# Feed-forward of a hybrid decoder layer: sum rows on another queue, scaling in place, other PSUM banks at the start of the second pair

## The chip, the core and the metric

The kernel runs on one core of one Trainium2 chip. The core has five engines that run their own instruction streams and meet through semaphores: TensorE (PE, matmuls), VectorE (DVE), ScalarE (ACT), GpSimd (POOL) and SyncE (SP). Each engine works in the order of its own program. SP and POOL here mostly issue transfers (DMAs). The metric is device time in microseconds, from the executions' own clock; lower is better. All values are float32.

## The reference, cut to what matters

One decoder layer works on a prompt of 2048 tokens and on 8 x 4 sample tokens. Two parallel branches (a gated linear recurrence and sliding-window attention) are merged by gates and multiplied by `w_o`; then comes the feed-forward, which is where the change lies, and a last norm:

```python
x = x + m @ w_o
h2 = _rmsnorm(x, n2)
x = x + jnp.square(jax.nn.relu(h2 @ w_ff1)) @ w_ff2
...
y_prompt = _rmsnorm(xp, normf_w)
y_sample = _rmsnorm(xs, normf_w)
```

Here x is tokens x 1024, `w_ff1` is 1024 x 4096 and `w_ff2` 4096 x 1024; `_rmsnorm` divides each token's row by the root of its mean square and multiplies by a weight.

## The kernel before

**Blocks and pairs.** The tokens stand in four blocks, features on the 128 partitions, tokens along the row. Two neighbouring blocks make a pair, and the feed-forward works on pairs: pair 0 with 512 columns per block (one chunk), pair 1 with 528 (two chunks of 264). The stages run one after another: projections and both branches of all blocks, `w_o` (tile `wob`), then for pair 0 the first feed-forward product (f1) and the second (f2), then f1 and f2 of pair 1.

**Seven products.** Both feed-forward matrices are multiplied by Strassen's scheme: the two blocks of a pair are the rows and the two halves of the features the columns of a 2 x 2 matrix. It needs the input halves A11, A12, A22 and four sums of them, S1 to S4. The function `ff_sums` makes the sums: for each of four row groups k it loads the pieces a11, a21, a12, a22 (from the DRAM buffers h2d, already normed, and x1d, not yet scaled) into one tile `xo`, scales what came from x1d (L598), writes one of the scaled pieces back to h2d (L600), forms s1, s2, s3, s4 with four DVE operations (L605 to L608) and stores them to the DRAM buffers dS (L610). The next k uses the same `xo`. For pair 1 this is done inside f2 of pair 0, in its second step. Its loads are L594 (from h2d) and L596 (from x1d); where a piece lies in both buffers there are two loads.

**Split numbers.** Every operand is split into a high and a low part, an ACT cast (L151, L257) and a DVE subtraction (L152, L258), and each product is three matmuls: high by high, high by low, low by high (L264 to L266 in f1, L1580 to L1582 in f2). So a weight tile such as `lw2T` goes DMA, ACT cast to `hw2T`, DVE subtraction in place, PE.

**f1.** `strassen_T` runs over 16 pairs of weight columns; each with each chunk is a `Unit`. Six units (pair 0) or ten (pair 1) begin ahead with two products (`a`: tiles fB, fC), and after each a list of `hooks` adds other work. Then every unit takes its remaining products (`b`, `c`), which use weights w1T and the sums. A unit's PSUM banks come from one of two rings of two banks, mm or tp; units 0 and 1 take mm, 2 and 3 tp, and so on. In pair 0 the norm of the last block (`Norm.stat`, tile `n_fb`: eight PE transposes of a sum of squares, a DVE reduction, a POOL power; then `spread`) is among the work that lies beside the first units. In pair 1 the hooks finish the output of pair 0's second block: squares, the statistic (`n_y`, PSUM ring hg), `spread`, and `Fin.out`, which scales eight rows of y by the norm (L1441) and writes them out (L1442, POOL's queue). There `f1.o` gives the scaled rows two buffers of their own, `fx_o`. The last of these hooks also loads S4, into the operand slot in which y stands, and `mid` splits it after unit 0's `b`.

**f2.** The second product has seven steps of four groups g; a group takes two weight tiles (`rw2B` or `lw2T`, L1558, SP's queue), one stored activation (`f2A` or `f2S`, L1574, SP's queue), and, in pair 0, 48 matmuls. After each step DVE adds the PSUM banks to y (L1587). For pair 0 the last step uses the hg and mm rings.

**What sets the order.** A scheduler in the kernel's framework takes instructions by priority and data dependences, within each engine; `pin` keeps an instruction in the order in which the program states it. The order on an engine is then fixed, and an instruction whose semaphore is not there holds up all behind it on that engine. This holds for transfers too: SP's queue carries weights, activations and the loads of `ff_sums` in one order; POOL's queue carries the stores and the loads of S1 to S4 (L615).

Of the kernel before, what the change touches and what calls it, by code (L numbers as in the profile page):

```python
# [16 lines left out]
P = 128  # L17
# [26 lines left out]
def tile_hybrid_step(  # L44
# [163 lines left out]

    def stat(rs, sq, n, name, ring=tp_ps):

        w = WT[n]
        nt = n // w
        for t0, ln in chunks_of(n):
            ps = ring(f"n_{name}_{t0}")[0:w].rearrange("p (c e) -> p c e", e=P)[:, 0:ln // w]
            for i in range(ln // w):
                nc.tensor.transpose(ps[:, i], sq[:, t0 + i * w:t0 + (i + 1) * w], ident)
            nc.vector.tensor_reduce(rs[:, t0 // w:(t0 + ln) // w], ps, AX.X, ALU.add)
        nc.vector.tensor_scalar(rs, rs, 1.0 / D, EPS, ALU.mult, ALU.add)
        nc.gpsimd.tensor_tensor(rs, rs, negh[0:w].broadcast_to([w, nt]), ALU.pow)
# [11 lines left out]
    class Norm:  # L231


        def __init__(u, tmp, n, w, name):
            u.tmp, u.n, u.w, u.N, u.acc = tmp, n, w, name, None
            u.rs, u.ring = carry_rs[0:WT[n], 0:n // WT[n]], tp_ps

# [9 lines left out]
        def stat(u):  # L247
            stat(u.rs, u.acc, u.n, u.N, u.ring)

# [60 lines left out]
    class Unit:  # L310


        def __init__(u, idx, w, t0, ln, A, st, fin):
            u.n, u.w, u.t0, u.ln, u.N = w.n, w.ops, t0, ln, f"{w.N}_{t0}"
            u.free = False
            u.ring, u.pair, u.A, u.st_, u.fin = (mm_ps, tp_ps)[idx // 2 % 2], w, A, st, fin

# [56 lines left out]

    def strassen_T(N, npairs, src, chunks, A, st, fin, ahead, early, mid, free, wt):
        ws = [Wpair(N, n, src, wt) for n in range(npairs)]
        nch = len(chunks)
        units = [Unit(i, ws[i // nch], *chunks[i % nch], A, st, fin) for i in range(npairs * nch)]
        if free:
# [205 lines left out]
    def ff_sums(b, v, r, k, loaded=False, q=nc.gpsimd):  # L585
# [4 lines left out]
        for x, (r0, c0) in zip(r, () if loaded else ((0, 0), (4, 0), (0, Th), (4, Th))):  # L590
            rows = slice((r0 + k) * P, (r0 + k + 1) * P)
            cut = min(max(raw0 - c0, 0), Th) if b == nsb - 1 else Th
            if cut:
                nc.sync.dma_start(x[:, 0:cut], h2d[b][rows, c0:c0 + cut])  # L594
            if cut < Th:
                nc.sync.dma_start(x[:, cut:Th], x1d[b][rows, c0 + cut:c0 + Th])  # L596
                i = c0 + cut - raw0
                nc.vector.scalar_tensor_tensor(x[:, cut:Th], x[:, cut:Th], n2c[:, r0 + k:r0 + k + 1], carry[:, i:i + Th - cut], ALU.mult, ALU.mult)  # L598
            if b == nsb - 1 and r0 and c0:
                nc.gpsimd.dma_start(h2d[b][rows, c0:c0 + Th], x)  # L600
# [31 lines left out]
    for bi in range(nblk):  # L632
# [774 lines left out]
        if last_b:  # L1407
            n2.ring = sw_ps
        late += [n2.stat, n2.spread] + ([] if last_b else [h2_out])
# [35 lines left out]
    for sb in range(nsb):  # L1445
# [13 lines left out]
        with tc.tile_pool(name=f"f1_{sb}", bufs=1, reuse_waits="tile") as fp:  # L1459
# [13 lines left out]
            else:  # L1473
                f1.x = lambda r: carry[:, 0:f1.ln] if r in ("acc", "rb") else fp.tile([P, f1.ln], F32, tag="fs", bufs=2, name=f"fx_{r}")
                f1.ns = lambda name: carry_rs
                f1.o = lambda: f1.x("o")
                hooks = [[lambda: f1.sq(0, 1, 2, 3)], [lambda: f1.sq(4, 5, 6, 7)], late_ops[0:2] + [f1.stat], late_ops[2:4], [f1.spread], [lambda: f1.out(0, 1, 2, 3)],
# [8 lines left out]
            def mid(u):  # L1486
                for f in s4_load:
                    f(u.c12)

# [3 lines left out]
            def f1_fin(u, blk, x, ps=None):  # L1493
# [12 lines left out]
                for o, y_ in (("A11", u.c11), ("A12", u.c12), ("A22", u.c22), ("S1", s1), ("S2", s2), ("S3", s3), ("S4", s4)):  # L1506
# [4 lines left out]
                       lambda ln, name: fp.tile([P, ln], F32, tag="st", bufs=12 * len(chunks), name=name),  # L1511
                       f1_fin, 6 if len(chunks) == 1 else 10, early, mid, True, lambda dt, name: fp.tile([P, 1024], dt, tag="we", bufs=2, name=name))

# [236 lines left out]
```

## Time and profile before

| | |
|---|---|
| median of three runs | 2822.58 us (2820.04 to 2824.71) |
| profiled execution, first to last instruction | 2810.0 us |
| TensorE clock granted, mean | 0.993 |
| transfers | 487.60 MB, mean 174 GB/s |
| f1 of pair 0 | from about 1499 us |
| f2 of pair 0 | about 1810 to 2122 us |
| f1 of pair 1 | from 2124 us |

The profile is of one execution; for its time the page gives only the span from the first to the last instruction, and the runs' times include what lies before and after it. The views used are: the busy time of each engine; the chain of waits that ended last; the timeline (start, length, engine, line, operation, and in brackets the idle time before it and what ended it); the waits, summed by line and by what was waited for; and windows, which give each engine's busy time in a stretch. In a name such as `lw2T_021` the digits are pair, group and half. Tiles lose these digits in the trace's views.

### The profile page before, as it was taken

The page shows a single profiled execution, that of the slowest core. Times are in us where ns is not written, and L with a number is a line of the kernel's source. Part 1 is how long each engine was busy: PE and PEld are TensorE (multiplying, and loading weights), DVE is VectorE, ACT ScalarE, POOL GpSimd, SP SyncE. Part 2 cuts the span into 40 slices and gives each one's busy share as a digit, 9 for nine tenths or more (in the row PEclk, how much of TensorE's full clock was granted, in tenths as well). Part 3 has the DMA queues.
Part 4 walks back from the last instruction along what each step waited for, and adds up shares of the span by engine and source line. Part 5 has one row for each costly group of instructions (what it writes and reads, how often), then busy time and mean ns, then how long its engine had stood idle before and what let it go on. Part 6 is the DMA issues. An engine that isn't in the chain of part 4 may idle for free.

```text
span 2810.0 us, 50089 instructions
## 1 busy us (share of the span) xinstructions
PE 2730.1 (97%) x20053; PEld 2403.9 (86%) x20053; DVE 1791.2 (64%) x2905; ACT 1110.0 (40%) x2070; POOL 490.9 (17%) x782
## 2 busy tenths in 40 slices
PE   8999999999999999899999999999999999999998
PEld 7778888788899977677898888878888999999998
DVE  5675746746774385637667777765567777654556
ACT  4542445423344353335334333434344233343332
POOL 1100211002300102320231221220012343320001
PEclk9999999999999999999999999999999999999999
DMA  5237662377743424652365544796566444485553
GB/s 190 75 103 237 208 198 76 97 242 256 251 126 115 144 76 149 219 160 67 105 210 184 181 145 150 265 317 222 190 200 215 147 161 135 155 291 184 189 187 119
DMA packets 344481, 487.60 MB, mean 174 GB/s; under 512 B 23432, under 2 KB 220824, under 8 KB 344248
## 3 DMA queue, kind: packets, MB, share of 16 engines
q1 hardware_dynamic: 289112, 329.10, 37.5%
q0 software_dynamic: 42880, 140.22, 13.8%
q10 hardware_dynamic: 12256, 15.08, 1.5%
q8 instruction: 157, 2.57, 0.4%
q14 instruction: 76, 0.62, 0.1%
HBM read 353.64 MB, written 130.68 MB: 172 GB/s over the span
## 4 chain that ended last, share of the span: by engine, by line
PE 78%; DMA 6%; DVE 6%; issue 5%; ACT 2%; POOL 2%; SPq 0%; POOLq 0%; DVEq 0%; ACTq 0%
PE f L1581 6%; PE f L1582 6%; PE f L1580 6%; PE fB_f L264 4%; PE fB_f L266 3%; PE fB_f L265 3%; PE fD_f L264 2%; PE fD_f L266 2%; PE fD_f L265 2%; PE ps_hfb L684 2%; PE fB_z L264 1%; PE fB_z L266 1%; PE fB_z L265 1%; PE wob L1390 1%; PE gab L166 1%
## 5 line engine op out<-in xcount | busy, mean ns | idle before, releaser
L1582 PE MATMUL f<-f2S,lw2T 128*128 128x264 f32 (+1 forms) x576 | 184.4, 320 | 2.0 <-DVE lw2T L152 2.0
L1580 PE MATMUL f<-f2S,hw2T 128*128 128x264 f32 (+1 forms) x576 | 184.5, 320 | 1.6 <-ACT hw2T L151 1.6
L1581 PE MATMUL f<-f2S,hw2T 128*128 128x264 f32 (+1 forms) x576 | 184.0, 319 | 0.0
L264 PE MATMUL fB_f<-S,w1T_f 128*128 128x264 f32 (+1 forms) x384 | 123.2, 322 | 3.1 <-ACT c_f L327 2.2
L152 DVE TENSOR_TENSOR lw2T<-lw2T,hw2T 128x1024 fp32r<-128x1024 f32 x64 | 78.2, 1224 | 69.7 <-ACT hw2T L151 68.8
L265 PE MATMUL fB_f<-S,w1T_f 128*128 128x264 f32 (+1 forms) x384 | 122.5, 319 | 0.0
L1580 PE MATMUL f<-f2A,h_w2B 128*128 128x264 f32 (+1 forms) x384 | 122.4, 319 | 0.0
L1581 PE MATMUL f<-f2A,h_w2B 128*128 128x264 f32 (+1 forms) x384 | 122.3, 319 | 0.0
L1582 PE MATMUL f<-f2A,l_w2B 128*128 128x264 f32 (+1 forms) x384 | 122.3, 318 | 0.0
L266 PE MATMUL fB_f<-S,w1T_f 128*128 128x264 f32 (+1 forms) x384 | 122.0, 320 | 0.0
L151 ACT CAST hw2T<-lw2T 128x1024 fp32r<-128x1024 f32 x64 | 67.2, 1051 | 137.2 <-DMA lw2T<-w_T 137.2
L1582 PEld LDWEIGHTS f<-f2S,lw2T 128*128 128x128 f32 x576 | 108.4, 188 | 10.4 <-DVE lw2T L152 2.9
L1580 PEld LDWEIGHTS f<-f2S,hw2T 128*128 128x128 f32 x576 | 108.8, 189 | 9.9 <-ACT hw2T L151 2.4
L1388 PE MATMUL wob<-m_b,h_wob 128*128 128x512 f32 (+2 forms) x320 | 113.1, 353 | 3.2 <-ACT h_wob L257 3.2
L1390 PE MATMUL wob<-m_b,l_wob 128*128 128x512 f32 (+2 forms) x320 | 112.4, 353 | 3.0 <-DVE l_wob L258 2.8
L1581 PEld LDWEIGHTS f<-f2S,hw2T 128*128 128x128 f32 x576 | 108.8, 189 | 7.6
L1389 PE MATMUL wob<-m_b,h_wob 128*128 128x512 f32 (+2 forms) x320 | 112.5, 352 | 0.0
L152 DVE TENSOR_TENSOR f2S<-f2S 128x1024 fp32r<-128x1024 f32 (+1 forms) x64 | 78.9, 1240 | 41.3 <-ACT f2S L151 40.9
L257 ACT CAST w1T_f<-w1r_f 128x512 fp32r<-128x512 f32 x128 | 77.1, 619 | 69.7 <-DVE w1r_f L300 29.7
L258 DVE TENSOR_TENSOR w1T_f<-w1r_f,w1T_f 128x512 fp32r<-128x512 f32 x128 | 87.4, 688 | 26.0 <-ACT w1T_f L257 25.7
L1507 POOL DMA_DIRECT2D u_A<-c_f x106 | 57.4, 541 | 236.1 <-DVE c_f L1491 225.1
L1507 POOL DMA_DIRECT2D u_S<-s_f x144 | 77.7, 541 | 109.0 <-DVE s_f L1502 92.4
(845 smaller groups left out, 9256.8 us busy)
## 6 DMA issues: line engine op xcount, KB each, us to landing
w1r_f<-w_ff SPq DMA_DIRECT2D x64, 512.0 KB
lw2T<-w_T SPq DMA_DIRECT2D x64, 512.0 KB
rw2B<-w_ff SPq DMA_DIRECT2D x48, 512.0 KB
f2S<-u_S SPq DMA_DIRECT2D x32, 528.0 KB
ws<-w_ff SPq DMA_DIRECT2D x32, 512.0 KB
r_wob<-w_o SPq DMA_DIRECT2D x32, 512.0 KB
f2S<-u_S SPq DMA_DIRECT2D x32, 512.0 KB
u_S<-s_f POOLq DMA_DIRECT2D x96, 132.0 KB, 2.3
```

The costliest lines, as they stand in the source:

```text
L152: pin(nc.vector.tensor_tensor(lo, F(lo), F(hi), ALU.subtract), on)
L258: pin(nc.vector.tensor_tensor(dl, src, F(dh), ALU.subtract), on)
L264: nc.tensor.matmul(ps, wh, ah, start=(first and k == 0), stop=False, skip_group_check=not first)
L265: nc.tensor.matmul(ps, wh, al, start=False, stop=False, skip_group_check=not first)
L266: nc.tensor.matmul(ps, wl, ah, start=False, stop=(last and k == 3), skip_group_check=not first)
L1388: nc.tensor.matmul(p, wh, ah, start=(k == 0), stop=False)
L1389: nc.tensor.matmul(p, wh, al, start=False, stop=False)
L1390: nc.tensor.matmul(p, wl, ah, start=False, stop=(k == KD - 1))
L1507: nc.gpsimd.dma_start(us[o][u.n // 4][u.n % 4 * P:(u.n % 4 + 1) * P, u.t0:u.t0 + u.ln], y_)
L1580: nc.tensor.matmul(ps, wh, ah, start=first, stop=False, skip_group_check=cont)
L1581: nc.tensor.matmul(ps, wh, al, start=False, stop=False, skip_group_check=cont)
L1582: nc.tensor.matmul(ps, wl, ah, start=False, stop=lastk, skip_group_check=cont)
```

## The change

Five edits, of which two go together.

- The loads of `ff_sums` are issued on POOL's queue, not SP's.
- The transposes of the last block's statistic in pair 0 are pinned (`n2.on`).
- `f1.o` goes: `Fin.out` scales pair 0's second block in place, in y, and writes y out.
- In pair 1 the units take the two PSUM rings the other way round (`flip`): units 0 and 1 take tp, 2 and 3 mm.
- The splits of S4 in pair 1 are pinned (`on=True`).

```diff
-    def stat(rs, sq, n, name, ring=tp_ps):
+    def stat(rs, sq, n, name, ring=tp_ps, on=False):
...
-                nc.tensor.transpose(ps[:, i], sq[:, t0 + i * w:t0 + (i + 1) * w], ident)
+                pin(nc.tensor.transpose(ps[:, i], sq[:, t0 + i * w:t0 + (i + 1) * w], ident), on)
...
-            u.rs, u.ring = carry_rs[0:WT[n], 0:n // WT[n]], tp_ps
+            u.rs, u.ring, u.on = carry_rs[0:WT[n], 0:n // WT[n]], tp_ps, False
...
-            stat(u.rs, u.acc, u.n, u.N, u.ring)
+            stat(u.rs, u.acc, u.n, u.N, u.ring, u.on)
...
-            u.ring, u.pair, u.A, u.st_, u.fin = (mm_ps, tp_ps)[idx // 2 % 2], w, A, st, fin
+            u.ring, u.pair, u.A, u.st_, u.fin = (mm_ps, tp_ps)[(idx // 2 + flip) % 2], w, A, st, fin
...
             if cut:
-                nc.sync.dma_start(x[:, 0:cut], h2d[b][rows, c0:c0 + cut])
+                nc.gpsimd.dma_start(x[:, 0:cut], h2d[b][rows, c0:c0 + cut])
             if cut < Th:
-                nc.sync.dma_start(x[:, cut:Th], x1d[b][rows, c0 + cut:c0 + Th])
+                nc.gpsimd.dma_start(x[:, cut:Th], x1d[b][rows, c0 + cut:c0 + Th])
...
         if last_b:
-            n2.ring = sw_ps
+            n2.ring, n2.on = sw_ps, True
...
-                f1.o = lambda: f1.x("o")
...
             def mid(u):
                 for f in s4_load:
-                    f(u.c12)
+                    f(u.c12, on=True)
...
-                       f1_fin, 6 if len(chunks) == 1 else 10, early, mid, True, lambda dt, name: fp.tile([P, 1024], dt, tag="we", bufs=2, name=name))
+                       f1_fin, 6 if len(chunks) == 1 else 10, early, mid, True, lambda dt, name: fp.tile([P, 1024], dt, tag="we", bufs=2, name=name), sb)
```

The line that goes makes every line number behind it one lower in the changed kernel (L1506 there is L1507 before).

**The start of f1 of pair 0.** PE, from the last matmuls of `w_o` (`wob`) to unit 0 (`fB_f_0`, `fC_f_0`); `n_fb` is the statistic, - is before:

```order
 L1389 MATMUL wob_288_14941<-m_b_14230,h_wob_14934 128x256
 L1390 MATMUL wob_288_14941<-m_b_14230,l_wob_14935 128x256
-L216 MATMUL n_fb_0_15178<-ident,carry 68x128 x4
-L216 MATMUL n_fb_272_15184<-ident,carry 68x128 x4
 L264 MATMUL fB_f_0_0_15100<-A_0_14652,w1B_f_0_15093 128x512
 L265 MATMUL fB_f_0_0_15100<-A_0_14652,w1B_f_0_15093 128x512
 L264 MATMUL fC_f_0_0_15115<-A_0_14661,w1B_f_0_15097 128x512
```

The eight transposes leave this place. PE further on, between the end of unit 1's and the start of unit 2's products:

```order
 L265 MATMUL fC_f_1_0_15163<-A_0_14661,w1B_f_1_15145 128x512
 L266 MATMUL fC_f_1_0_15163<-A_0_14661,w1B_f_1_15145 128x512
+L216 MATMUL n_fb_0_15178<-ident,carry 68x128 x4
+L216 MATMUL n_fb_272_15184<-ident,carry 68x128 x4
 L264 MATMUL fB_f_2_0_15201<-A_0_14652,w1B_f_2_15194 128x512
 L265 MATMUL fB_f_2_0_15201<-A_0_14652,w1B_f_2_15194 128x512
```

They now stand two units later. The reductions on DVE and the power on POOL follow them.

**The second step of f2 of pair 0.** SP before, in the third and fourth group of the step (`lw2T_02`, `lw2T_03`: weights; `f2S`: activations; `xo`: the sum rows of k=2 and k=3):

```order
L1558 DMA lw2T_020_17953<-w_T_139 128x2x512
L1574 DMA f2S_0_18033<-u_S_3_0_15075 128x2x512 x2
L1558 DMA lw2T_021_17958<-w_T_139 128x2x512
L596 DMA xo_17493<-x1d_101 128x528
L594 DMA xo_17493<-h2d_103 128x512
L596 DMA xo_17493<-x1d_101 128x16
L596 DMA xo_17493<-x1d_101 128x528
L1558 DMA lw2T_030_18041<-w_T_139 128x2x512
L1574 DMA f2S_0_18102<-u_S_0_0_15084 128x2x512 x2
L1558 DMA lw2T_031_18046<-w_T_139 128x2x512
L594 DMA xo_17493<-h2d_103 128x512
L596 DMA xo_17493<-x1d_101 128x16
```

All L594 and L596 rows leave SP's queue (24 transfers), so weights follow activations there without a break. POOL now, at the change from k=1 to k=2 (`dS_1_108` to `111`: the stores of S1 to S4):

```order
L610 DMA dS_1_109<-xo_17493 128x528
L610 DMA dS_1_110<-xo_17493 128x528
L594 DMA xo_17493<-h2d_103 128x512
L596 DMA xo_17493<-x1d_101 128x16
L596 DMA xo_17493<-x1d_101 128x528 x2
L610 DMA dS_1_111<-xo_17493 128x528
L600 DMA h2d_103<-xo_17493 128x528
L594 DMA xo_17493<-h2d_103 128x512
L596 DMA xo_17493<-x1d_101 128x16
L610 DMA dS_1_108<-xo_17493 128x528
```

Before, POOL had only the L610 and L600 rows here. Now each load stands behind stores of the k before, and the last store of k=1 (`dS_1_111`) stands behind three loads of k=2. DVE before, around the low part of `lw2T_021`:

```order
L152 TENSOR_TENSOR lw2T_020_17953<-lw2T_020_17953,hw2T_020_17952 128x1024
L606 TENSOR_TENSOR xo_17493<-xo_17493 128x528
L152 TENSOR_TENSOR f2S_0_18033<-f2S_0_18033 128x1024
L607 TENSOR_TENSOR xo_17493<-xo_17493 128x528
L152 TENSOR_TENSOR f2S_0_18033<-f2S_0_18033 128x1024
L608 TENSOR_TENSOR xo_17493<-xo_17493 128x528
L152 TENSOR_TENSOR lw2T_021_17958<-lw2T_021_17958,hw2T_021_17957 128x1024
```

and in the changed kernel:

```order
L152 TENSOR_TENSOR lw2T_020_17953<-lw2T_020_17953,hw2T_020_17952 128x1024
L152 TENSOR_TENSOR f2S_0_18033<-f2S_0_18033 128x1024
L598 SCALAR_TENSOR_TENSOR xo_17493<-xo_17493,cols,carry 128x16
L607 TENSOR_TENSOR xo_17493<-xo_17493 128x528
L152 TENSOR_TENSOR f2S_0_18033<-f2S_0_18033 128x1024
L258 TENSOR_TENSOR A_1_17787<-xo_17493,A_1_17787 128x528
L152 TENSOR_TENSOR lw2T_021_17958<-lw2T_021_17958,hw2T_021_17957 128x1024
```

The scaling of a12's last columns (L598) and its split (L258) now stand ahead of `lw2T_021`; the fourth sum (L608) stands behind it. `lw2T_031` stands in the same way behind the L598 of k=3.

**The start of f1 of pair 1.** DVE before, at the scaling of y (L1441) among the products' first combinations (L342, tile c_f) of units 2 and 3:

```order
L1441 SCALAR_TENSOR_TENSOR fx_o<-y_0_17492,cols,carry 128x512 x2
L258 TENSOR_TENSOR w1T_f_0_20053<-w1r_f_0_20036,w1T_f_0_20053 128x512
L258 TENSOR_TENSOR w1T_f_0_20056<-w1r_f_0_20038,w1T_f_0_20056 128x512
L342 TENSOR_TENSOR c_f_2_264_19851<-fC_f_2_264_19852,p_f_2_264_19849 128x264
L297 TENSOR_TENSOR w1r_f_1_20194<-w1r_f_1_20194 128x4x128
L1491 SCALAR_TENSOR_TENSOR c_f_2_264_19851<-c_f_2_264_19851 128x264
L1441 SCALAR_TENSOR_TENSOR fx_o<-y_0_17492,cols,carry 128x512 x2
L342 TENSOR_TENSOR c_f_3_0_19903<-fC_f_3_0_19904,p_f_3_0_19901 128x264
```

and in the changed kernel:

```order
L1441 SCALAR_TENSOR_TENSOR y_0_17492<-y_0_17492,cols,carry 128x512 x3
L342 TENSOR_TENSOR c_f_2_264_19851<-fC_f_2_264_19852,p_f_2_264_19849 128x264
L1441 SCALAR_TENSOR_TENSOR y_0_17492<-y_0_17492,cols,carry 128x512
L1490 SCALAR_TENSOR_TENSOR c_f_2_264_19851<-c_f_2_264_19851 128x264
L1441 SCALAR_TENSOR_TENSOR y_0_17492<-y_0_17492,cols,carry 128x512 x3
L342 TENSOR_TENSOR c_f_3_0_19899<-fC_f_3_0_19900,p_f_3_0_19897 128x264
L1441 SCALAR_TENSOR_TENSOR y_0_17492<-y_0_17492,cols,carry 128x512
```

The eight scalings stand closer together and earlier; before, the last two came after the L342 of unit 4. On ACT the copy of unit 0's c22 and the casts of S4 change places: before the copy stands between the two casts of S4, now ahead of both.

More of the change, by code (lines that the diff above doesn't have):

```diff
@@ L310, in tile_hybrid_step, with __init__ @@
     class Unit:
-        def __init__(u, idx, w, t0, ln, A, st, fin):
+        def __init__(u, idx, w, t0, ln, A, st, fin, flip):
             u.n, u.w, u.t0, u.ln, u.N = w.n, w.ops, t0, ln, f"{w.N}_{t0}"
             u.free = False
-            u.ring, u.pair, u.A, u.st_, u.fin = (mm_ps, tp_ps)[idx // 2 % 2], w, A, st, fin
+            u.ring, u.pair, u.A, u.st_, u.fin = (mm_ps, tp_ps)[(idx // 2 + flip) % 2], w, A, st, fin
         def st(u, name):
@@ L373, in c, with strassen_T @@
             u.fin(u, "c12", u.c12)
-    def strassen_T(N, npairs, src, chunks, A, st, fin, ahead, early, mid, free, wt):
+    def strassen_T(N, npairs, src, chunks, A, st, fin, ahead, early, mid, free, wt, flip=0):
         ws = [Wpair(N, n, src, wt) for n in range(npairs)]
         nch = len(chunks)
-        units = [Unit(i, ws[i // nch], *chunks[i % nch], A, st, fin) for i in range(npairs * nch)]
+        units = [Unit(i, ws[i // nch], *chunks[i % nch], A, st, fin, flip) for i in range(npairs * nch)]
         if free:
```

## The prediction

> **What bounds the kernel now.** I read the busy times first, then the chain of work that ended last.
>
> ```profile
> span 2810.0 us, 50089 instructions
> PE 2730.1 (97%) x20053; PEld 2403.9 (86%) x20053; DVE 1791.2 (64%) x2905; ACT 1110.0 (40%) x2070; POOL 490.9 (17%) x782
> PE 78%; DMA 6%; DVE 6%; issue 5%; ACT 2%; POOL 2%; SPq 0%; POOLq 0%; DVEq 0%; ACTq 0%
> ```
>
> TensorE (PE) is busy for 97% of the span, so the end comes earlier only if one of PE's idle stretches closes, and later only if one opens. The diff removes no matmul and adds none. The sum is therefore made from PE's idle times at the three places where the order changes: the start of the first feed-forward product of pair 0 (near 1500 us, "A"), the second step of its second product (1820 to 1900, "B"), and the start of the first product of pair 1 (2120 to 2170, "C"). The windows view gives for each stretch its length, then PE, PEld, DVE, ACT and POOL busy (instructions), the granted clock, DMA share and GB/s:
>
> ```profile
> 1500.00:1520.00 20.00, 18.13 (x82) 14.49 (x83) 16.97 (x23) 15.99 (x24) 6.64 (x8) 1.00 0.86 273
> 1860.00:1880.00 20.00, 18.28 (x79) 14.54 (x79) 15.04 (x20) 7.17 (x8) 2.70 (x5) 0.99 0.81 276
> 1880.00:1900.00 20.00, 18.15 (x72) 14.22 (x72) 14.16 (x17) 9.31 (x10) 2.71 (x5) 0.92 1.00 359
> 1900.00:1920.00 20.00, 20.00 (x90) 16.57 (x89) 14.44 (x15) 9.46 (x11) 0.00 (x0) 1.00 0.76 269
> 2120.00:2140.00 20.00, 17.87 (x136) 16.92 (x136) 18.98 (x32) 11.90 (x23) 4.50 (x6) 1.00 0.57 177
> 2140.00:2160.00 20.00, 17.73 (x133) 17.52 (x132) 16.38 (x32) 6.18 (x13) 7.10 (x14) 0.91 0.60 203
> ```
>
> A full stretch of the second product holds 90 matmuls; the two at B hold 79 and 72. Besides the idle time there is a clock loss: 0.92 in 1880 to 1900 is worth 0.08 x 20 = 1.6 us, 0.91 in 2140 to 2160 is 0.09 x 20 = 1.8 us. I call such a loss a dip and price it at 1.7 us.
>
> **A, the pinned statistic.** The timeline of PE and ACT at the start of unit 0 (start, length, what; in brackets idle time and releaser), and a later statistic between matmuls:
>
> ```profile
> 1501.02 1.06 PE L216 MATMUL n_fb<-ident,carry 128*68 128x128 f32 x8 [2.02 <-DVE carry L245]
> 1501.99 1.14 ACT L257 CAST w1B_f<-w1r_f 128x512 fp32r<-128x512 f32 x2
> 1502.66 0.50 PE L264 MATMUL fB_f<-A,w1B_f 128*128 128x512 f32 x1 [0.58 <-ACT w1B_f L257]
> 2133.60 0.66 PE L216 MATMUL n_y<-ident,carry 128*128 128x128 f32 x4 [0.43 <-DVE carry L1427]
> 2134.01 0.37 PE L264 MATMUL fB_f<-A,w1B_f 128*128 128x264 f32 x1
> ```
>
> Before, the eight transposes stand ahead of unit 0. They fill 1.06 us of a stretch in which PE waits anyway: unit 0 goes at 1502.66, when ACT's cast of its weights is ready, and ACT's order up to that cast is the same in both kernels. So moving the transposes away starts nothing earlier. They now run after unit 1, among matmuls, where four cost 2134.01 - 2133.60 = 0.41 us, so eight cost **0.8 us**. Beyond that, PE is idle in one piece of 2.02 + 1.06 + 0.58 = 3.66 us. In this trace a dip followed PE's waits of 1.46 us (B) and 2.27 us (C), but not this 2.02 us, where the clock stays at 1.00. A wait longer than any of them is more likely than not followed by one, so I add 1.7: **A = +2.5 us**, bounds 0 (the eight fall into a wait of unit 1 or 2; a gain is excluded, since unit 0's start is set by the cast) and +2.6 (the larger dip).
>
> [...]
>
> **B, sum rows on POOL's queue.** Each k of the sums loads six pieces into one buffer set xo, waits on the stores that still read it, and DVE makes four sums that are stored. Before, these loads stand in SP's queue between the weights of the second product. What SP waited for in 1810 to 1900 (line, releaser, us, times, longest), when it issued lw2T_021, lw2T_030 and lw2T_031, when ACT cast 021 and 031, and PE's waits:
>
> ```profile
> SPq L594 <- DVE xo L607: 14.0, 2, 11.2
> SPq L594 <- DMA dS<-xo: 10.1, 2, 6.5
> SPq L596 <- DMA h2d<-xo: 9.5, 2, 8.9
> SPq L596 <- DMA dS<-xo: 4.4, 2, 2.5
> ...
> 1867.50 0.66 SPq L1558 DMA_DIRECT2D lw2T<-w_T  x1
> 1881.51 0.48 SPq L1558 DMA_DIRECT2D lw2T<-w_T  x1
> 1883.15 1.10 SPq L1558 DMA_DIRECT2D lw2T<-w_T  x1
> ...
> 1876.38 1.05 ACT L151 CAST hw2T<-lw2T 128x1024 fp32r<-128x1024 f32 x1 [0.66 <-DMA lw2T<-w_T]
> 1892.22 1.04 ACT L151 CAST hw2T<-lw2T 128x1024 fp32r<-128x1024 f32 x1 [1.39 <-DMA lw2T<-w_T]
> ...
> 1877.48 0.50 PE L1580 MATMUL f<-f2S,hw2T 128*128 128x512 f32 x1 [0.26 <-ACT hw2T L151]
> 1879.67 0.80 PE L1582 MATMUL f<-f2S,lw2T 128*128 128x512 f32 x1 [1.46 <-DVE lw2T L152]
> 1893.32 0.50 PE L1580 MATMUL f<-f2S,hw2T 128*128 128x512 f32 x1 [1.32 <-ACT hw2T L151]
> 1894.58 0.50 PE L1582 MATMUL f<-f2S,lw2T 128*128 128x512 f32 x1 [0.53 <-DVE lw2T L152]
> ```
>
> SP stood 38.0 us behind buffer waits of the sums, so weights went out late, ACT cast them late, and PE lost 0.26 + 1.46 + 1.32 + 0.53 = 3.57 us and a dip, 5.3 us in all. Free of the sums, SP can issue these weights as soon as their buffers are free, and the two waits on ACT's casts should go. But the last step of a weight, its low part on DVE, still stands in DVE's order behind work of the sums: lw2T_021 now stands behind the third sum of k=2 and a split, lw2T_031 behind a scaling for k=3. And the sums now go through one in-order queue, where stores stand behind loads that wait for earlier stores to land:
>
> ```profile
> 1877.02 0.54 POOL L610 DMA_DIRECT2D dS<-xo  x1 [1.21 <-DVE xo L607]
> ...
> DMA to landing us min/median/max: 3.2/5.6/6.7
> ...
> L598 DVE SCALAR_TENSOR_TENSOR xo<-xo,cols,carry x16: 226/499/771, 1834.1 to 1894.4; 128x16 f32<-128x16 f32 x8, 128x528 f32<-128x528 f32 x8
> L605 DVE TENSOR_TENSOR xo<-xo x4: 701/706/709, 1840.5 to 1884.7; 128x528 f32<-128x528 f32 x4
> L594 SPq DMA_DIRECT2D xo<-h2d x8: 319/332/645, 1825.4 to 1884.4; - x8
> ...
> 1827.02 4.24 POOL L1626 DMA_DIRECT2D y<-x1d  x8 [3.44 <-DMA u_S<-s_f]
> ```
>
> The second row is the landing of the stores dS. A round for one k (a store lands, a load lands, sums, next store) holds two landings, six issues on POOL at 0.54 = 3.2 us (24 issues in all, 13 us on an engine that is 17% busy), and DVE's scaling and three sums, 0.77 + 3 x 0.71 = 2.9 us: 12.5 us with landings of 3.2, 17.3 with 5.6. The third sum of k=2 ended just before 1877.0 (L607 released that store). If rounds stay as they were, it now ends some 2 us later or more: the first loads went from 1825.4 on, and now stand behind six y loads on POOL (4.24 / 8 = 0.53 us each, the last five from 1827.02), to about 1829.7; DVE's first scaling was not before 1834.1 in any case. Behind that sum a split now stands ahead of lw2T_021. I expect lw2T_021 some 2 us later than before, and lw2T_031 1 us later than PE then wants it, against the two ACT waits of 0.26 + 1.32 = 1.58 us that go. So **B = +1.5 us**. Bounds: -5.3 (all gone), and +8 (three rounds longer by the 2.2 us that two landings at 6.7 instead of 5.6 cost, 6.6, and the 1.5 taken).
>
> **C, start of pair 1.** PE's waits in 2120 to 2240 by line, the DVE wait of the scaling L1441, and the rows around the S4 cast:
>
> ```profile
> PE fC_f L264 <- DVE c_f L342: 2.3, 1, 2.3
> PE fB_f L264 <- ACT c_f L327: 2.2, 2, 2.0
> PE fB_f L264 <- DVE y L1587: 1.7, 1, 1.7
> ...
>   DMA out_yT<-fx_o: 3.6, 3
> ...
> 2155.50 0.43 DVE L342 TENSOR_TENSOR c_f<-fC_f,p_f 128x264 f32<-128x264 f32 x1
> ...
> 2165.14 1.07 ACT L151 CAST S<-S 128x1056 fp32r<-128x1056 f32 x1 [1.05 <-DMA S<-dS]
> 2166.12 0.37 ACT L327 COPY c_f<-fB_f 128x264 f32<-128x264 f32 x1
> ```
>
> Other banks: unit 0 waits 1.7 us for the last eviction out of the mm banks (L1587). In the tp banks it needn't. But the statistic n_y stands three units on and waits for DVE, which is 18.98 of 20 us busy there and works on regardless; PE comes 1.7 us earlier to it and waits 0.43 + 1.7 there. That edit is worth **0**, bounds -1.7 and +1.7 (a dip after the longer wait). In place: DVE stood 3.6 us for writes that still read the two fx_o buffers, and L342 stood behind. Without them L342 runs some 4 us earlier, ahead of PE's demand, so its 2.3 us and the dip behind it go: **-4.1**. S4 pinned: the copy at 2166.12 that released PE's 2.0 us stood behind a cast waiting for the S4 load. It now stands ahead. I take -2.0 for that and +1.0 for the S4 products that come later, because S4's slot is free only when the writes of y have landed (that load had no such wait): **-1.0**, bounds -2 and +3. C = 0 - 4.1 - 1.0 = **-5.1**.
>
> **The sum.** +2.5 + 1.5 - 5.1 = -1.1. The profiled execution's span is 2810.0, 12.6 below the median 2822.58 of the runs; I take that difference as what lies around the span. 2808.9 + 12.6 = **2821.5 us**.
>
> **Rivals.**
> 1. SP's release is worth all of B. With landings near 3.2 us a round is up to 4.8 us shorter than with 5.6; the two rounds up to the third sum of k=2 then win far more than the late start costs, and all of 5.3 us goes. For it: 38.0 us of SP waits in front of late weights. Against it: DMA share 1.00 in 1880 to 1900. With A at 0.8 and C at -5.1: -9.6, **2813.0**.
> 2. POOL's queue becomes the bound (slower). Its in-order mix of loads and stores makes lw2T_021 and lw2T_031 late by three long rounds: B = +8, and S4, on the same queue behind the writes of y, at its bound of +3 instead of -1.0: 2.5 + 8 - 4.1 + 3 = +9.4, **2832.0**. It decides once a store takes over about 6 us to land in 1840 to 1890; DMA share 1.00 speaks for it.
> 3. No dip at A, as weighed above: 0.8 + 1.5 - 5.1 = -2.8, **2819.8**.
> 4. The move to POOL does not do what it says: the transfers, not SP's place in line, set when weights come, B = 0: 2.5 - 5.1 = -2.6, **2820.0**. [...]
>
> **How the numbers follow.** Forecast 0.28, rival 1 0.28, rival 2 0.20, rivals 3 and 4 0.12 each. A measurement of this kernel can tell about 0.2%, 5.6 us, from no change: faster is below 2816.9, slower above 2828.2. Forecast and rivals 3 and 4 lie within (0.52), rival 1 is faster (0.28), rival 2 slower (0.20). The range takes in rival 1 and the forecast's neighbours, with half of rival 2's way: 2811 to 2831.
>
> **What would show it.** A: the clock in 1500 to 1510 and one wait of 3.7 us ahead of unit 0. B: PE's waits at hw2T and lw2T in 1875 to 1900; their releaser tells ACT's late cast from DVE's. C: unit 0 starts without a wait, n_y waits about 2.1 us, no wait for L342, and what the first S4 product waits for. I am wrong if PE loses time outside these places, or if landings on POOL's queue differ from those of before.

## The result and the profile after

The changed kernel takes 2827.43 us in the median of 21 runs (2817.54 to 2833.09), the kernel before 2821.46 in 21 runs taken beside it (2813.08 to 2828.14). The ratio is 1.0020, 95% interval 1.0012 to 1.0028: **5.6 us slower, between 3.4 and 7.9**. The forecast was -1.1 us.

The page of the changed kernel: span, busy times, and the chain that ended last.

```profile
span 2828.3 us, 50096 instructions
PE 2741.3 (97%) x20053; PEld 2413.7 (85%) x20053; DVE 1788.7 (63%) x2905; ACT 1107.3 (39%) x2070; POOL 505.5 (18%) x806
PE 80%; DMA 7%; DVE 5%; issue 4%; ACT 3%; POOL 1%; SPq 0%; POOLq 0%; ACTq 0%; DVEq 0%
```

The spans differ by 18.3 us, three times the result. The two profiles aren't comparable as wholes: the last `wob` matmul starts at 1498.7 before and at 1509.5 after, in a part of the program that is the same in both. So I compare stages by the starts of matmuls in the timeline of PE: A runs from the first matmul of f1 to the first of f2, B from the first to the last of f2, C from there to the first of f2 of pair 1, and the rest to the last matmul of the program.

| stage | before | after | change | forecast |
|---|---|---|---|---|
| f1 of pair 0 (A) | 307.75 | 311.86 | +4.1 | +2.5 |
| f2 of pair 0 (B) | 311.68 | 316.26 | +4.6 | +1.5 |
| turn to pair 1 and its f1 (C) | 344.37 | 341.50 | -2.9 | -5.1 |
| rest | 335.74 | 337.43 | +1.7 | 0 |

The windows of the changed kernel at these places (columns as before; its stages run 10.7 us later at A and 15 to 20 us later at B and C):

```profile
1500.00:1520.00 20.00, 16.33 (x95) 14.38 (x94) 12.53 (x16) 10.77 (x14) 5.42 (x8) 0.83 0.65 212
1880.00:1900.00 20.00, 13.88 (x57) 10.37 (x56) 12.89 (x19) 5.06 (x6) 5.87 (x11) 0.87 0.91 303
1900.00:1920.00 20.00, 19.42 (x74) 15.48 (x74) 15.51 (x20) 9.09 (x11) 4.83 (x9) 0.87 0.72 253
2140.00:2160.00 20.00, 18.12 (x143) 17.58 (x142) 18.98 (x34) 11.90 (x24) 5.03 (x7) 1.00 0.57 180
2160.00:2180.00 20.00, 20.00 (x165) 19.81 (x164) 19.60 (x40) 6.94 (x15) 9.10 (x17) 1.00 0.79 254
```

At A the clock is 0.83, where it was 1.00. At B two windows hold 57 and 74 of 90 matmuls, at clock 0.87 in both; before, it was 79 and 72, and one dip. At C the second window is full, where before it had a dip and 133 matmuls.

The timeline of the changed kernel shows what stands behind these numbers. At A, PE's first matmul of unit 0:

```profile
1513.40 0.80 PE L264 MATMUL fB_f<-A,w1B_f 128*128 128x512 f32 x1 [3.67 <-ACT w1B_f L257]
```

At B, rows of PE, ACT, DVE and POOL put one below the other:

```profile
1897.82 0.80 PE L1579 MATMUL f<-f2S,hw2T 128*128 128x512 f32 x1 [5.01 <-ACT hw2T L151]
...
1896.19 0.63 ACT L257 CAST A<-xo 128x528 fp32r<-128x528 f32 x1 [10.13 <-DVE xo L598]
1896.72 1.04 ACT L151 CAST hw2T<-lw2T 128x1024 fp32r<-128x1024 f32 x1
...
1895.92 0.23 DVE L598 SCALAR_TENSOR_TENSOR xo<-xo,cols,carry 128x16 f32<-128x16 f32 x1 [3.24 <-DMA xo<-x1d]
...
1882.70 0.55 POOL L610 DMA_DIRECT2D dS<-xo  x1 [2.20 <-DVE xo L598]
1890.32 0.54 POOL L594 DMA_DIRECT2D xo<-h2d  x1 [1.65 <-DMA dS<-xo]
1890.86 0.54 POOL L596 DMA_DIRECT2D xo<-x1d  x1
```

Read upwards, this is the 5.01 us. POOL issued the last load of a12 for k=2 at 1890.86, behind a wait for the fourth sum's store of k=1, which had gone out at 1882.70. The load landed when DVE's L598 could start, 1895.92. ACT's split of a12 waited for that (10.13 us idle), and the cast of `hw2T_021` stood behind the split on ACT, with no wait of its own: it started as soon as the split was through. SP had that weight in good time: the last `lw2T` of the step went out at 1880.82, and what SP waited for in 1826 to 1920 is no longer a buffer of the sums but PE's use of the weight buffers:

```profile
SPq L1557 <- PE f L1581: 58.8, 7, 18.1
```

At C, PE's waits in 2138 to 2260:

```profile
PE n_y L216 <- DVE carry L1427: 1.9, 1, 1.9
PE fB_f L264 <- DVE c_f L329: 1.5, 2, 1.2
PE fD_f L264 <- ACT S L151: 0.9, 1, 0.9
PE fB_f L264 <- ACT c_f L327: 0.7, 1, 0.7
PE fD_f L265 <- DVE S L152: 0.4, 1, 0.4
```

The waits for L1587 (1.7), L342 (2.3) and the 2.0 us one for L327 are gone, n_y waits 1.9, and the first S4 products wait 0.9 + 0.4.

### The profile page after: what moved, and what is told of

Same layout as the page of the kernel before. It is cut to its first block, busy times and chain, and to the rows that moved or that the text cites. A ratio compares the mean times of both kernels' runs of the same rounds, so it can differ in the third digit from the quotient of the medians.

```text
span 2828.3 us, 50096 instructions
## 1 busy us (share of the span) xinstructions
PE 2741.3 (97%) x20053; PEld 2413.7 (85%) x20053; DVE 1788.7 (63%) x2905; ACT 1107.3 (39%) x2070; POOL 505.5 (18%) x806
## 4 chain that ended last, share of the span: by engine, by line
PE 80%; DMA 7%; DVE 5%; issue 4%; ACT 3%; POOL 1%; SPq 0%; POOLq 0%; ACTq 0%; DVEq 0%
PE f L1580 6%; PE f L1581 6%; PE f L1579 6%; PE fB_f L264 4%; PE fB_f L266 4%; PE fB_f L265 4%; PE ps_hfb L684 2%; PE fD_f L264 2%; PE fD_f L265 2%; PE fD_f L266 2%; PE wob L1388 2%; PE wob L1390 2%; PE wob L1389 2%; PE fB_z L264 1%; PE fB_z L266 1%
## 5 line engine op out<-in xcount | busy, mean ns | idle before, releaser
L1581 PEld LDWEIGHTS f<-f2S,lw2T 128*128 128x128 f32 x576 | 108.8, 189 | 10.8 <-DVE lw2T L152 3.3
L258 DVE TENSOR_TENSOR w1T_f<-w1r_f,w1T_f 128x512 fp32r<-128x512 f32 x128 | 87.1, 686 | 28.2 <-ACT w1T_f L257 28.2
L1506 POOL DMA_DIRECT2D u_S<-s_f x144 | 77.7, 541 | 118.5 <-DVE s_f L1501 95.9
L1506 POOL DMA_DIRECT2D u_A<-c_f x106 | 57.3, 541 | 227.8 <-DVE c_f L1490 220.2
```

Source lines behind the costliest of these rows:

```text
L258: pin(nc.vector.tensor_tensor(dl, src, F(dh), ALU.subtract), on)
L1506: nc.gpsimd.dma_start(us[o][u.n // 4][u.n % 4 * P:(u.n % 4 + 1) * P, u.t0:u.t0 + u.ln], y_)
L1581: nc.tensor.matmul(ps, wl, ah, start=False, stop=lastk, skip_group_check=cont)
```

## Experiments

All times are against the kernel before, run beside each kernel on the same chip. The last three columns come from one profile of each kernel: f2 is the stage B, the next is PE's waits for weights in it, the last the time in it at half clock (granted 0.5; the changed kernel has 0.50 from 1895.0 to 1905.0), all in us.

| run | ratio, 95% interval | us | f2 | waits for weights | at half clock |
|---|---|---|---|---|---|
| kernel before | 1 | 0 | 311.7 | 3.6 | 3.4 |
| changed kernel | 1.0020, 1.0012 to 1.0028 | +5.6 | 316.3 | 6.7 | 10.2 |
| e1 statistic free | 1.0014, 1.0004 to 1.0024 | +4.0 | 320.2 | 10.8 | 10.2 |
| e2 loads on SP | 0.9992, 0.9979 to 1.0005 | -2.3 | 312.5 | 4.3 | 3.4 |
| e3 only pair 1's edits | 0.9992, 0.9978 to 1.0007 | -2.3 | 313.0 | 5.3 | 3.4 |
| e4 only POOL loads | 1.0034, 1.0021 to 1.0048 | +9.6 | 316.9 | 8.0 | 7.2 |
| x1 POOL, second a12 | 1.0033, 1.0019 to 1.0047 | +9.3 | 318.6 | 7.6 | 10.2 |
| x2 POOL, stores on SP | 1.0010, 0.9998 to 1.0021 | +2.8 | 313.5 | 5.9 | 0 |
| x3 pair 1's edits, wide xo | 0.9980, 0.9967 to 0.9993 | -5.6 | 310.3 | 3.0 | 3.4 |
| x4 only in place | 0.9987, 0.9974 to 0.9999 | -3.7 | 311.6 | 3.4 | 3.4 |
| x5 POOL, wide xo | 1.0020, 1.0006 to 1.0033 | +5.6 | 314.4 | 6.6 | 3.4 |
| x6 in place, wide xo | 0.9985, 0.9974 to 0.9996 | -4.2 | 311.5 | 2.8 | 6.8 |
| x7 only the statistic | 1.0017, 1.0004 to 1.0029 | +4.8 | 312.9 | 4.7 | 3.4 |
| x8 only wide xo | 0.9997, 0.9987 to 1.0007 | -0.8 | 309.1 | 3.2 | 0 |
| y1 POOL, sums pinned | 0.9972, 0.9958 to 0.9986 | -7.9 | 305.4 | 0 | 0 |
| y2 pair 1's edits, sums pinned | 0.9976, 0.9965 to 0.9987 | -6.8 | 308.9 | 0 | 0 |
| y3 POOL, pair 1's edits, sums pinned | 0.9958, 0.9942 to 0.9974 | -11.8 | 305.4 | 0 | 0 |

**Which part costs.** Four kernels take the change apart. e1 is the changed kernel with

```diff
-            n2.ring, n2.on = sw_ps, True
+            n2.ring = sw_ps
```

> The changed kernel with the last block's statistic not pinned, all else as changed. Theory (the parts add up: statistic +4.1 us in f1 of pair 0, of which 0.8 are the eight transposes among matmuls and up to 3.4 a clock dip after one idle stretch of 3.7 us; queue +4.6 us in f2 of pair 0; start of pair 1 -2.9): about +2 us against the kernel before, the wait ahead of unit 0 again split into 2.0 and 0.6 with the clock at 1.00 in the 20 us that follow, and the 5 us wait for hw2T in f2 of pair 0 still there. Rival (the statistic costs only its 0.8 us, dips come at random): about +5 us, and a dip as likely as in the changed kernel.

e2 is the changed kernel with both loads of `ff_sums` on `nc.sync` again, e3 has both of these, and e4 is the kernel before with the two loads on `nc.gpsimd` and nothing else.

> The changed kernel with the loads of the sum rows back on SP's queue, all else as changed. Theory (parts add up): about +1 us against the kernel before; f2 of pair 0 lasts 311 to 313 us from its first to its last matmul (before 311.7, changed 316.3), no wait for hw2T above 2 us there; ahead of unit 0 one wait of 3.7 us and a dip. Rival (the queue is not what costs, the transfers of the sums are late on any queue): f2 of pair 0 stays near 316 us.

> The kernel before with only the edits at the start of pair 1 (in place, other banks, S4 pinned). Theory: -3 us against the kernel before, all of it between the last matmul of f2 of pair 0 and the first of f2 of pair 1 (before 344.4 us, changed 341.5). Rival (the gain there is a clock dip that happened to fall out, not the waits): 0 us, with that stretch between 341 and 346 depending on dips.

> The kernel before with only the loads of the sum rows moved to POOL's queue. Theory (ACT's and DVE's weight work stands in order behind a piece of the sums whose load waits for the store of the fourth sum of the k before): +4.6 us against the kernel before, f2 of pair 0 about 316 us, PE waits about 5 us for hw2T_021. Rival (that wait comes from the shift that the other edits give to this stage, or from one slow transfer in the profiled execution): 0 us, f2 near 312 us.

POOL's queue is the whole loss: +9.6 us alone, and without it the change is -2.3. The stage of e4 is as expected (316.9) and its time is twice that (+4.6 expected); the profiles don't show where the rest goes. e1 missed its +2 with +4.0, and the clock behind unit 0 wasn't full (below). e2 came out at -2.3 (up to +1.4) where +1 was expected, and has a wait for hw2T just above the 2 us. PE's waits for weights in e4, and in e2:

```profile
PE f L1580 <- ACT hw2T L151: 4.4, 1, 4.4
PE f L1582 <- DVE lw2T L152: 3.6, 4, 1.5
```

```profile
PE f L1579 <- ACT hw2T L151: 2.3, 1, 2.3
PE f L1581 <- DVE lw2T L152: 2.0, 2, 1.5
```

The wait of 4.4 to 5.0 us for hw2T is in all three profiles with loads on POOL in which nothing else of the sums was touched (the changed kernel, e1, e4), so it isn't one slow transfer. Pair 1's edits (e3) are -2.3 with an interval that takes in 0; their stage is 6.0 us shorter in that profile (338.4 against 344.4).

**What POOL's queue costs by.** The rows at B blame the buffer of a12. x1 gives a12 a second place for every other k (on e4):

```diff
-y1, xo = raw8(6, Th, f"y1_{sb}"), fp.tile([P, 6, Ths[sb + 1]], F32, name=f"xo{sb}")
+y1, xo = raw8(6, Th, f"y1_{sb}"), fp.tile([P, 7, Ths[sb + 1]], F32, name=f"xo{sb}")
...
-todo = [lambda k=k: ff_sums(sb + 1, nv, [xo[:, i] for i in range(6)], k) for k in range(4)]
+todo = [lambda k=k: ff_sums(sb + 1, nv, [xo[:, i] for i in (0, (1, 6)[k % 2], 2, 3, 4, 5)], k) for k in range(4)]
```

> The kernel before with the loads of the sum rows on POOL's queue, and a seventh row in xo, so that the a12 pieces of k=1 and k=3 have a place of their own and the load of a12 need not wait for the store of the fourth sum of the k before. Theory (PE's 4.4 to 5.0 us wait for hw2T_021 is ACT's cast of that weight standing behind the cast of a12 of k=2, whose load waited for the store of the fourth sum of k=1): the wait for hw2T falls below 1.5 us, f2 of pair 0 lasts 311 to 313 us, and the time is within 3 us of the kernel before (loads on POOL alone: +9.6). Rival (POOL's queue is late as a whole, by its place in line and slower transfers): the wait stays above 3 us, f2 near 316 us, +8 us.

```profile
PE f L1582 <- DVE lw2T L152: 7.6, 4, 2.3
```

My theory fell. The wait for hw2T is gone, and the cost isn't: four waits for the low parts on DVE took its place. x2 (on e4) sends the stores of the sums to SP's queue, `ff_sums(..., k, q=nc.sync)`; x5 (on e4) gives all four pieces a second place, ten rows:

```diff
+todo = [lambda k=k: ff_sums(sb + 1, nv, [xo[:, i] for i in ((0, 8)[k % 2], (1, 6)[k % 2], (2, 7)[k % 2], (3, 9)[k % 2], 4, 5)], k) for k in range(4)]
```

> The kernel before with the loads of the sum rows on POOL's queue and the stores of the four sums on SP's queue, so that no load stands behind a store of the k before, and no store behind a load. Rival (mixing loads and stores in one in-order queue is what costs): f2 of pair 0 back at 311 to 313 us, 0 us against the kernel before. Theory (the cost is the order on ACT and DVE together with the buffer a12): ACT's cast of a12 of k=2 still stands ahead of that of hw2T_021, so a wait of 3 to 5 us for hw2T remains and f2 lasts 315 to 318 us; SP's weights now also stand behind stores.

> The kernel before with the loads of the sum rows on POOL's queue and xo with ten rows (a second place for all four pieces). A second place for a12 alone did not help. Theory (a load that stands in one queue with the stores whose landing it awaits makes each round of the sums a store's landing plus a load's landing long; it is not POOL's issue or its transfers): with no such wait f2 of pair 0 lasts 309 to 312 us (loads on POOL alone: 316.9), and the time is within 3 us of the kernel before. Rival (POOL's queue itself is late: 0.54 us an issue, eight transfers in flight, y loads ahead): f2 stays at 315 us or more, +6 us or more.

PE's waits for weights in f2 of x2, then of x5:

```profile
PE f L1582 <- DVE lw2T L152: 5.9, 4, 2.4
```

```profile
PE f L1582 <- DVE lw2T L152: 6.6, 4, 2.8
```

Each removes a part of the cost (x2 6.8 us of 9.6, with an f2 near what the rival expected; x5 4.0, between theory and rival, with an interval that overlaps that of e4), and neither removes the waits on DVE: 5.9 and 6.6 us. So neither the mix of loads and stores in one queue nor the buffer is the end of it. What the six kernels with loads on POOL so far have in common is that DVE, or ACT, does sum work ahead of a weight's split. In x5 it looks like this on DVE, ahead of PE's wait of 2.76 us at 1884.95:

```profile
1880.38 0.24 DVE L598 SCALAR_TENSOR_TENSOR xo<-xo,cols,carry 128x16 f32<-128x16 f32 x1 [2.73 <-DMA xo<-x1d]
...
1883.68 1.22 DVE L152 TENSOR_TENSOR lw2T<-lw2T,hw2T 128x1024 fp32r<-128x1024 f32 x1
```

DVE stood idle for a load of the sums with the weight's low part behind it. y1 changes the order of that work and no instruction (the order on POOL changes with it: most stores of a k now stand ahead of the loads of the next). It pins the sum work, so that each k stands where the program states it, behind the weight splits of its groups (on e4; `split_k` takes `on` and hands it to `split_out`):

```diff
-                nc.vector.scalar_tensor_tensor(x[:, cut:Th], ...)
+                pin(nc.vector.scalar_tensor_tensor(x[:, cut:Th], ...))
...
-            split_k(v, k, a11)
-            split_k(v, 4 + k, a12)
-        pin(tt(s1, a21, a22, ALU.add), loaded)
+            split_k(v, k, a11, True)
+            split_k(v, 4 + k, a12, True)
+        pin(tt(s1, a21, a22, ALU.add))
```

and the other three sums likewise.

> The kernel before with the loads of the sum rows on POOL's queue, and the scalings, splits and four sums kept in program order, where each k stands behind the weight splits of its two groups on ACT and DVE. Theory (the cost of the move is paid where weight splits stand in order behind sum work whose loads are late; the lateness by itself costs nothing): PE's waits for hw2T and lw2T in f2 of pair 0 go below 1 us in all, f2 lasts 309 to 311 us (loads on POOL alone: 316.9), and the time is at or below the kernel before (-3 to 0 us; loads on POOL alone: +9.6). Rival (POOL's queue also delays something else, such as the y loads and stores, or takes bandwidth from the weights): +4 us or more.

-7.9 us, more than expected, and no wait of PE's for a weight. On DVE the scaling of a k (L598) now stands behind the weight's low part, and it never waits for a load, because by then the load has landed:

```profile
1866.47 1.22 DVE L152 TENSOR_TENSOR lw2T<-lw2T,hw2T 128x1024 fp32r<-128x1024 f32 x1 [1.27 <-ACT hw2T L151]
1867.62 1.73 DVE L598 SCALAR_TENSOR_TENSOR xo<-xo,cols,carry 128x16 f32<-128x16 f32 x4
```

The windows of y1:

```profile
1860.00:1880.00 20.00, 20.00 (x90) 16.55 (x89) 14.90 (x18) 8.84 (x10) 4.92 (x10) 1.00 0.83 293
1880.00:1900.00 20.00, 20.00 (x90) 16.57 (x89) 15.30 (x20) 9.48 (x10) 4.60 (x9) 1.00 0.76 263
1900.00:1920.00 20.00, 20.00 (x90) 16.57 (x89) 12.51 (x18) 9.27 (x10) 3.62 (x8) 1.00 0.90 319
```

All three are full at clock 1.00. And the sums of y1 are later, not earlier. The third sums (L607) of before, of the changed kernel and of y1:

```profile
L607 DVE TENSOR_TENSOR xo<-xo x4: 701/702/703, 1841.8 to 1886.0; 128x528 f32<-128x528 f32 x4
```

```profile
L607 DVE TENSOR_TENSOR xo<-xo x4: 700/701/701, 1857.5 to 1909.7; 128x528 f32<-128x528 f32 x4
```

```profile
L607 DVE TENSOR_TENSOR xo<-xo x4: 701/702/704, 1850.1 to 1919.4; 128x528 f32<-128x528 f32 x4
```

From the start of f2 (1810.4, 1825.3, 1811.8) the last comes after 76, 84 and 108 us. Lateness of the sums costs nothing here; standing ahead of a weight's split costs. So the cost of the move is the order on ACT and DVE. y1 also has another order on POOL, but x2 and x5, which changed what POOL's loads stand behind, left the waits, and the sums of y1 are not earlier for it.

**Pair 1.** x4 is the kernel before without the line `f1.o = lambda: f1.x("o")`.

> The kernel before with only the scaling in place at the start of pair 1. Theory (the gain there is the wait of DVE for the writes of fx_o that goes, 2.3 us and its dip on PE): -2 to -4 us against the kernel before, the wait of PE for L342 gone, the 1.7 us wait for the banks ahead of unit 0 still there. Rival (the gain comes from the other banks and the pinned S4): 0 us.

-3.7 us. PE's waits in 2120 to 2240 of x4, then the longest of e3:

```profile
PE fB_f L264 <- ACT c_f L327: 4.1, 2, 3.6
PE fB_f L264 <- DVE c_f L329: 1.7, 2, 1.3
PE fB_f L264 <- DVE y L1586: 1.3, 1, 1.3
PE n_y L216 <- DVE carry L1427: 0.4, 1, 0.4
```

```profile
PE n_y L216 <- DVE carry L1427: 1.9, 1, 1.9
PE fB_f L264 <- DVE c_f L329: 1.6, 2, 1.3
PE fB_f L264 <- ACT c_f L327: 1.1, 1, 1.1
```

In place alone removes the wait for L342; part of it comes back at the copy that stands behind the S4 casts (L327, 3.6 us). In e3, with S4 pinned and the other banks, that wait is gone, the 1.3 us for the banks (L1586) are gone, and n_y waits 1.9 us instead of 0.4. The times of x4 and e3 can't be told apart (-3.7 and -2.3).

**The statistic.** x7 is the kernel before with the pinned transposes alone (the lines with `on` in `stat`, `Norm` and `n2`).

> The kernel before with only the last block's statistic pinned. Theory: +2.5 us (0.8 of transposes among matmuls, 1.7 of a dip more often or longer); ahead of unit 0 one wait of 3.7 us, the clock at half for 3.4 to 6.8 us behind it. Rival (dips come behind this place with or without the pin, as in four unpinned runs out of five): +1 us.

+4.8, between 1.1 and 8.2, which takes in the theory and not quite the rival; the changed kernel against e1 gives +1.7. Ten microseconds around unit 0's start of x7, then of e1, where the statistic is free (the time at half clock is twice what the clock lacks to 1.00, times the length: 6.8 and 3.4 us):

```profile
1504.00:1514.00 10.00, 7.10 (x18) 5.26 (x19) 8.11 (x10) 8.35 (x11) 3.43 (x5) 0.66 1.02 334
```

```profile
1508.00:1518.00 10.00, 8.45 (x34) 6.73 (x35) 7.81 (x11) 8.11 (x12) 5.02 (x6) 0.83 1.00 342
```

**Versions.** x3 is e3 with the ten rows of x5, x6 is x4 with them, x8 is the kernel before with them.

> The kernel before with the edits at the start of pair 1 (in place, other banks, S4 pinned), loads on SP as before, and xo with ten rows, so that all four pieces have a second place for every other k. Theory: without the waits of loads for stores of the k before, SP issues the weights in time; the 3.6 us of waits and the dip in f2 of pair 0 go (f2 309 to 310 us, before 311.7), and with the -2 to -4 us of the edits at pair 1 the time is 7 us below the kernel before. Rival (weights are late because transfers are, the DMA engines being full): f2 stays at 312 us, -3 us.

> The kernel before with only the scaling in place and xo with ten rows, loads on SP. Theory (these two hold all the gain; other banks and the pinned S4 add nothing): -7 us against the kernel before, like the run that also has the other banks and S4 pinned (-7.4 by medians). Rival (the other banks carry part of it): -4 us.

> The kernel before with only xo widened to ten rows, loads on SP. Theory: f2 of pair 0 309.5 to 310.5 us against 311.7, and -3 us in all (the difference between the two runs with the edits at pair 1, with and without the ten rows, is -2.9 by medians). Rival: 0 us, that difference being noise.

The ten rows alone are unclear (-0.8, between -3.7 and +2.0, where -3 was expected), and x3 and x6 can't be told apart. y2 and y3 pin the sum work as y1 does, on e3 and on e1.

> The kernel before with the edits at the start of pair 1 (in place, other banks, S4 pinned) and the sum work kept in program order, loads on SP. Theory: the sum work is no longer ahead of the weights' splits, but the loads still stand in SP's queue ahead of weight loads; PE's waits for the weights shrink but need not go, f2 309.5 to 312 us, and -5 to -8 us against the kernel before. Rival (the waits of before come from SP's queue alone): f2 stays at 312 to 313 us, -3 us.

> The changed kernel without the pinned statistic and with the sum work kept in program order (loads on POOL, in place, other banks, S4 pinned). Theory: the gains of both stages add: -6 to -9 us against the kernel before, f2 of pair 0 309 to 311 us, start of pair 1 some 4 us shorter than before. Rival (POOL's queue costs as it did): +4 us, like the changed kernel without the pinned statistic (+4.0).

y3 beats both kernels, and by more than expected: 2808.62 us in the median of six runs, ratio 0.9958 (0.9942 to 0.9974). It is the changed kernel without the pinned statistic and with pinned sums. Two of its windows at B and C:

```profile
1880.00:1900.00 20.00, 20.00 (x90) 16.57 (x89) 12.96 (x18) 8.51 (x10) 3.22 (x6) 1.00 0.89 308
2140.00:2160.00 20.00, 20.00 (x164) 19.81 (x163) 19.59 (x39) 6.78 (x15) 9.29 (x17) 1.00 0.78 250
```

In y2, with the loads on SP, the weights' waits go as well. So the waits of the kernel before went without another queue, though SP still stood 38.3 us behind buffer waits of the sums (1820 to 1920). But a wait of 3.3 us for an eviction on DVE (L1586) comes, and f2 is 3.6 us longer than in y1 and y3. That eviction stands behind a weight's low part, for which DVE waited 3.94 us for ACT's cast of `h_w2B`, and ACT 9.22 us for the load, which SP had issued at 1904.42, behind loads of the sums. So by the profiles POOL's queue is the better place, once the order is right, by some 3.6 us. The times agree (y3 is 5.0 us below y2) but their intervals overlap.

## Why the prediction was wrong

**A was right in its steps.** One wait of 3.67 us stands ahead of unit 0 (forecast 3.66), the transposes went among matmuls, and a dip comes with it (granted 0.50 from 1513.0 to 1519.0). The size: the stage lasts 311.5 us in the mean of three profiles with the pin, and 309.2 in 14 without it, +2.3, against +2.5. 0.7 us of the +4.1 in the table are a longer wait at the end of f1 (1.35 us for L359, 0.61 before), outside the places that I had named. My ground for the dip was thin. The 1.00 of the one profile of before was the exception: 13 of the 14 profiles without the pin have the clock at half behind this place, nine of them for 3.4 us and four for 6.8. All three with the pin have 6.8. So the pin adds in the mean 2.7 us at half clock (6.8 against 4.1), which is 1.3 us, to a dip that is there anyway, where I had added a whole dip of 1.7; that the sum came out as near as +2.3 is in part luck. It speaks against rival 3, which had no dip added, without excluding it: the clock is at half for 6.8 us in three of three with the pin, against 3.4 or none in ten of the 14 without it, and three profiles aren't many.

**B is the step that failed.** Its term was +1.5; the stage shows +5.5 (317.8 in the mean of the three kernels with loads on POOL that leave the sums as they are, 312.3 in the five such with loads on SP), and the times +6 to +10 (e4 +9.6; the changed kernel against e2 7.9; e1 against e3 6.2). Two sentences of it were wrong:

- "the two waits on ACT's casts should go". They became one of 5.0 us. I took the weight's arrival as the end of its wait, because in the rows of before the casts waited for DMA. I went by the new order on DVE and left out that on ACT. There the split of a12 for k=2 had moved ahead of the cast of `hw2T_021`: the weight was there, and its cast stood behind sum work.
- "If rounds stay as they were, it now ends some 2 us later or more", and from it "I expect lw2T_021 some 2 us later than before". The rounds did not stay as they were. The stores of POOL's timeline show it, first the last store of k=0 of before:

```profile
1845.31 0.54 POOL L610 DMA_DIRECT2D dS<-xo  x1 [1.96 <-DVE xo L608]
```

  and of the changed kernel the last three stores of k=0 and that of the third sum of k=2, with the time to landing of all its stores:

```profile
1857.91 1.78 POOL L610 DMA_DIRECT2D dS<-xo  x3 [0.69 <-DVE xo L606]
...
1897.06 0.54 POOL L610 DMA_DIRECT2D dS<-xo  x1 [4.06 <-DVE xo L607]
...
DMA to landing us min/median/max: 2.7/4.7/8.7
```

  From the last store of k=0 to the third sum's of k=2 it is 31.7 us before (1845.3 to 1877.0) and 37.9 after (1859.2, the third of its row, to 1897.1), 3.1 us more for each of two rounds, though the last store of k=0 was not late at all (34.9 us after the start of f2 before, 33.9 after). On POOL the loads of k=1 start behind that store (1859.68) and wait 4.12 and 1.11 us more for landings, where SP had issued the first of them at 1842.58, ahead of it. I had this as rival 2, with a price for B (+8) that is near the times, and with a condition that isn't what decides: stores that take over 6 us to land. The stores land in 4.7 us in the median, less than the 5.6 of before. The one that the load of a12 waited for (1882.70) did take 7.1 us, but that is 1.5 us more than 5.6, of a wait of 5.0, and in y1 stores take up to 8.1 us (5.5 in the median) without a wait of PE's.

Behind both is one error: I priced the move as lateness of the sums, with its lateness passed on to the weights by DVE. y1 shows that lateness alone is free and that the order decides. Rival 1, SP's release worth all of B (-5.3), is only partly alive under that condition: y1 and y3 have an f2 that is 6.3 us shorter than before (305.4 against 311.7), but by one profile each the pins alone take 4.1 us of f2 with the loads on SP (313.0 in e3, 308.9 in y2), and the move then takes 3.6 (305.4 in y3). So a part of what I had put down to SP's queue was the order on ACT and DVE. Rival 4, by which the move would do nothing, falls: it costs 5.5 us of f2 in the one order and saves 3.6 in the other.

**C was right, as far as the profiles show.** Unit 0 starts without a wait, n_y waits 1.9 us (forecast 2.1), the wait for L342 and its dip are gone, the 2.0 us for the copy are gone, and 1.3 us come back at the S4 products (forecast 1.0). The turn and f1 of pair 1 last 340.8 us in the mean of seven profiles with all three edits and 345.5 in eight with none: -4.6, forecast -5.1. In place alone is -2.1 by two profiles, -3.7 by the times. By the times all of C (e3) is -2.3, between -6.2 and +2.0, which leaves the size open.

**The sum.** With +2.3, +5.5 and -4.6 it is +3.2, just below the measured 3.4 to 7.9; with B as the times have it, +4 to +7. The profiles settle the places, and not the last two microseconds.

**The base.** I took 12.6 us as lying around the span. It is 1.7: a later execution whose own time is known took 2808.44 us with a span of 2806.7 (y3). The profiled execution of before was one of the shortest. The forecast of a difference is not touched by it.

## What to carry to other kernels

When loads move to another queue, look up every engine that handles the data on either side, and ask what has been put behind it there: a scheduler that sets the order of every engine can put the moved work ahead of something that the bottleneck needs, as it did here on ACT and DVE. A wait whose row names a DMA is not gone when the DMA comes early; the next engine in the chain has its own order. And work with much time to spare (the sums are read in the next product) went best, in y1 to y3, pinned behind the work that has none.

## What the runs showed of the hardware

The clock behind an idle stretch is not the same from run to run, and one profile can't say whether a place has a dip: after the 2.0 us wait, the 1.1 us of transposes and about 0.5 us more at A, the clock stayed full in one execution and fell to half for 3.4 or 6.8 us in 13. In f2 of the six kernels with loads on POOL and the sums not pinned, all with waits of 6 to 11 us, it was at half for 10.2 us in three (the changed kernel, e1, x1), for 7.2 in e4, 3.4 in x5 and not at all in x2. So, with half of that time as my estimate of its cost, it took up to 5.1 us on top of such waits, and nothing in x2. One sum fits f2 in all 17 profiles within 2 us: the 305.4 us of y1 and y3, which have neither waits nor half clock, and PE's waits, and half of the time at half clock. The windows of x1:

```profile
1860.00:1880.00 20.00, 17.70 (x72) 14.12 (x71) 15.54 (x24) 6.02 (x7) 6.47 (x12) 0.91 0.91 328
1880.00:1900.00 20.00, 15.71 (x66) 12.06 (x65) 14.72 (x20) 10.76 (x12) 7.02 (x13) 0.98 0.81 281
1900.00:1920.00 20.00, 18.97 (x74) 14.97 (x73) 15.05 (x16) 7.10 (x8) 0.00 (x0) 0.85 0.57 197
```

The clock lacks 0.09, 0.02 and 0.15 of 20 us each; twice that is some 10 us at half clock. It came there though no wait of PE's in 1826 to 1925 was longer than 2.3 us, and in x2 a wait of 2.4 us brought none. So here the half clock can come with waits no longer than that, and does not always.
